# A routed expert layer on one core: gate and up with the weights standing, 160 tokens moving

## The chip, the cores and the metric

The kernel runs on one core of a Trainium2 chip. The metric is the device time of one execution in microseconds. Each number is the median of several runs; one further execution is profiled, and the views shown are of that one.

## The reference

One layer of a decoder on 2048 tokens of width 1024, in float32. What matters here is the middle step, the mixture of experts: 32 experts in 4 groups; each token takes its best group and in it its best two experts. An expert is a gated MLP with a hidden width of 512.

```python
def expert_block(args):
    xblk, e = args
    hdn = jax.nn.silu(xblk @ w_gate[e]) * (xblk @ w_up[e])
    return hdn @ w_down[e]
```

With 2 x 2048 assignments over 32 experts, a mean of 128 tokens falls to one expert. Before it come attention and a short convolution with their projections; after it a gated per-layer embedding and the last norm.

## The kernel before

Everything is computed to nearly float32 precision by splitting each operand into a high part and a low part (both fp32r): `split` makes the high part on ScalarE (L65) and the low part, the difference, on VectorE (L66). A product is then three matmuls: high x high, high x low, low x high (`mm3`, L73 to L75). TensorE holds one operand, loaded by its weight loader (PEld), and moves the other past it.

The stages follow one another: the input projections (`project`), attention (`attention`), the output projection with the router (`mix_out`), a loop for far tokens (`far_experts`), the experts (`experts`), and the rest (`finish`). The order of the work in the expert stage is written out by hand (manual schedule): each engine takes its instructions in the order of the program.

**Experts.** Each expert's three weight matrices are 12 units of 512 KB: units 0 to 3 are gate, 4 to 7 up, 8 to 11 down. SyncE loads units into a ring of 12 raw buffers (L754), a whole expert ahead. `next_unit` splits the next raw unit into a ring of 10 split units (`uh`, `ul`), which frees the raw buffer for the next load. A split waits until TensorE is done with the unit that held its place.

The program holds two bodies for each expert, chosen at run time by the expert's count of tokens: `block(e, True)` for more than 128 tokens, `block(e, False)` for up to 128. The text calls them the wide and the near body. Tokens are listed by expert and rank; GpSimd (POOL) gathers the first 128 rows of an expert into `xg0` and, where the count is over 128, up to 64 further rows into `xg1` (L1220, one gather each). `trans` transposes the first rows (4 transposes to a PSUM tile, L1229) and splits them to `xh` and `xl`. This is done for the next expert within the body of the present one, after units 8 and 9.

In both bodies the tokens stand in TensorE and the weights move: gate by 512 columns, up by 256 (two halves `f` of the hidden width), down by 512, three matmuls for each block. In the wide body the further rows come besides: their transposes at the start of the body (L1356), high and low part side by side as one standing operand of 128 columns, and two matmuls for each block (L1285, L1286); low is added to high afterwards, through `half` (L1250, L1251).

For each half of the hidden width VectorE multiplies up with silu(gate) (`u`, L1299; `sum`, L1296), TensorE transposes the product (L1306, two transposes for the first rows and two for the further ones), and it is split to `hh`, `hl` or `hs` for the down products. `store` copies the result out of PSUM and POOL writes it to `yd`: 128 rows (L1324), and 64 rows (L1322) in the wide body.

Tokens with a rank of 192 and over would go through `far_experts`, a loop over blocks of 128 rows that is entered only if there are any. It scatters its lists with 32 indirect DMAs and adds the results with 32 gathers.

The choice and the order of an expert:

```python
if e + 1 < E:
    with tc.If(self.counts[e + 1] > 128):
        self.gather(e + 1, 1)
n = self.nsplit, self.nload
with tc.If(self.counts[e] > 128) as c:
    block(e, True)
self.nsplit, self.nload = n
with c.Else():
    block(e, False)
```

Of the kernel before, what the change touches and what calls it, by code (L numbers as in the profile page):

```python
# [32 lines left out]

R1 = E * 128
R2 = R1 + E * 64
FAR = 192
# [14 lines left out]
class Kernel:  # L51
# [716 lines left out]

    def next_unit(self, pool=False):
        k = self.nsplit - 12 - 12 * E  # L770
        self.split_unit(self.gcol[:, k:k + 1] if k >= 0 else None, pool)
        self.unit_loads()

    def mix_out(self, st):
# [124 lines left out]
        def route(t0, n):  # L899
# [90 lines left out]
            yield V.tensor_scalar(u1, e_, -64.0, float(R1 - 128), op0=OP.mult, op1=OP.add)  # L990
# [122 lines left out]
        for e in range(2):  # L1113
            self.gather(e, 0)
        self.gather(0, 1)
# [28 lines left out]
        for k in range(2):  # L1144
            self.trans(0, 4 * k, pst)

# [56 lines left out]
    def expert_tiles(self):  # L1203
# [4 lines left out]
        self.idx1 = cp.tile([64, E], I32, name="idx1")  # L1208
        self.xT = [self.xt_pair(cp, 0)]
        self.xg = [[cp.tile([n, D], F32, name=f"xg{r}{i}") for i in range(2)] for r, n in enumerate((128, 64))]  # L1210
# [4 lines left out]
    def xt_pair(self, p, i):  # L1215
        return [p.tile([128, KD, 128], F32R, name=f"{n}{i}") for n in ("xh", "xl")]
# [8 lines left out]
    def trans(self, e, kk, pst):  # L1225
        xh, xl = self.xT[e % 2]
# [3 lines left out]
        self.split(xh[:, kk:kk + 4], xl[:, kk:kk + 4], ps)  # L1230
# [6 lines left out]
    def experts(self, st):  # L1237
        tc, nc = self.tc, self.nc
        V, mm = nc.vector, nc.tensor.matmul
        self.xT.append(self.xt_pair(self.pool(self.est, "e_x1", 1), 1))  # L1240
# [3 lines left out]
        self.banks = [psm.tile([128, 512], F32, name=f"bank{i}") for i in range(6)]  # L1244

        def half(ps, n, out=None):

            lo = wk.tile([64, 512], F32, name="lo", bufs=1)
            r = wk.tile([64, 256], F32, name="sum", bufs=1) if out is None else out
            nc.scalar.activation(lo[:, :n], ps[64:128, :n], AF.Copy)  # L1250
            V.tensor_tensor(r[:, :n], ps[0:64, :n], lo[:, :n], op=OP.add)  # L1251
            return r

        def block(e, more):

            xh, xl = self.xT[e % 2]
            pg, pg1, pu, pu1 = self.banks[0], self.banks[1], self.banks[2::2], self.banks[3::2]
            ys, y1 = self.banks[2:4], self.banks[4:6]
            unit = lambda j: self.units[(10 + 12 * e + j) % NSPLIT]
            hh = wk.tile([128, 4, 128], F32R, name="hh", bufs=1)  # L1260
            hl = wk.tile([128, 4, 128], F32R, name="hl", bufs=1)
            if more:
                xs = wk.tile([128, KD, 2, 64], F32R, name="xs", bufs=1)
                hs = wk.tile([128, 4, 2, 64], F32R, name="hs", bufs=1)

            def free():

                self.next_unit()

            def prods(j, r):  # L1270

                uh, ul = unit(j)
                if j < 4:
                    n, ks, nk, out = 512, (2 * j, 2 * j + 1), KD, [(pg, pg1)[r]]
                elif j < 8:
                    f, i = divmod(j - 4, 2)
                    n, ks, nk, out = 256, range(4 * i, 4 * i + 4), KD, [(pu, pu1)[r][f]]
                else:
                    n, ks, nk, out = 512, (j - 8, j - 8), 4, (ys, y1)[r]
                for i, k in enumerate(ks):  # L1280
                    ps = out[i % len(out)][:, :n]
                    wh, wl = uh[:, i * n:i * n + n], ul[:, i * n:i * n + n]
                    if r:
                        s = xs[:, k] if j < 8 else hs[:, k]
                        mm(ps, s, wh, start=k == 0, stop=False)  # L1285
                        mm(ps, s, wl, start=False, stop=k == nk - 1)  # L1286
                    else:
                        s = (xh[:, k], xl[:, k]) if j < 8 else (hh[:, k], hl[:, k])
                        self.mm3(ps, [(*s, wh, wl)], start=k == 0, stop=k == nk - 1)

            def hidden(f, r):

                fs = slice(f * 256, f * 256 + 256)
                if r:
                    u = half(pu1[f], 256)[:, :256]
                    V.tensor_tensor(u, u, sl1[:, fs], op=OP.mult)  # L1296
                else:
                    u = wk.tile([128, 256], F32, name="u", bufs=1)
                    V.tensor_tensor(u, pu[f][:, :256], sl[:, fs], op=OP.mult)  # L1299
                return u  # L1300

            def hidden_trans(f, r, u):
                n = 64 if r else 128
                ps = self.pst.tile([128, 4, 128], F32, name="tr")[:, :2, :n]
                for k in range(2):
                    nc.tensor.transpose(ps[:, k], u[:, k * 128:k * 128 + 128], self.ident[:n, :n])  # L1306
                K = slice(2 * f, 2 * f + 2)
                if r:
                    self.split(hs[:, K, 0], hs[:, K, 1], ps)
                else:  # L1310
                    self.split(hh[:, K], hl[:, K], ps)

            def store(r):
# [14 lines left out]
            def first(j):  # L1328
# [9 lines left out]
                if j == 11:  # L1338
                    store(0)
# [419 lines left out]
```

## Time and profile before

| | before |
|---|---|
| median of 3 runs | 2375.61 us (2374.02 to 2383.3) |
| the profiled execution, its own time | 2378.32 us |
| its span in the profile | 2376.6 us |
| expert stage, first store to last | 1297.3 to 2136.6 us |
| experts with the wide body / the near body | 16 / 16 |

The span runs from the first to the last instruction of the profile; the own time holds a little around it. In the views, PE is TensorE's matmuls, PEld its weight loads, DVE VectorE, ACT ScalarE, POOL GpSimd and SP SyncE. A matmul's recorded duration includes its way through the pipeline, so that records of one stream overlap; the distance between two starts tells the pace.

### The profile page before, as it was taken

Reading aid. Unit: us, or ns where it says so; the run is one execution under the profiler, and the core shown is the slowest. Engines: PE = TensorE matmul, PEld = TensorE weight load, DVE = VectorE, ACT = ScalarE, POOL = GpSimd, SP = SyncE. Lnnn points to the kernel's source line nnn. Section 1 sums busy time; section 2 is a strip of 40 time slices with the busy share of each in tenths; the row PEclk is TensorE's granted clock in tenths of the full one; section 3 lists DMA queues with packets and bytes.
Section 4 is the critical chain, followed back from the end, with each engine's and each line's share of the span. In section 5 each row is a group of like instructions: output and inputs, shape, how many; then the busy total and the mean of one; then the engine's idle time right before and its main releaser. Section 6 shows DMA issues by size and latency. Waiting matters only on the chain. (4 is left out here: it accounts for less than half of the span.)

```text
span 2376.6 us, 34881 instructions
## 1 busy us (share of the span) xinstructions
PE 2262.7 (95%) x12058; PEld 1869.0 (79%) x12058; DVE 1700.2 (72%) x3109; ACT 1341.3 (56%) x2407; POOL 481.8 (20%) x570
## 2 busy tenths in 40 slices
PE   7999999999999999999988999999999999999997
PEld 6888888888888888778866877787787777778775
DVE  5756666648888888866775777668667776766887
ACT  5334334328888888732236676667556666665443
POOL 0121212022333333401131000101001111003432
PEclk9999999999999999999999999999999999999999
DMA  7363635464556443566647899779777896873552
GB/s 226 100 224 95 223 94 180 110 197 128 134 129 130 90 90 78 133 207 203 205 151 239 293 331 320 230 229 360 230 235 268 288 323 227 290 253 131 173 194 96
DMA packets 297850, 465.68 MB, mean 196 GB/s; under 512 B 27609, under 2 KB 197634, under 8 KB 297602
## 3 DMA queue, kind: packets, MB, share of 16 engines
q1 hardware_dynamic: 253696, 333.43, 45.8%
q0 software_dynamic: 36384, 105.53, 13.6%
q10 hardware_dynamic: 7522, 23.61, 2.7%
q8 instruction: 133, 2.18, 0.4%
q14 instruction: 115, 0.94, 0.2%
HBM read 369.04 MB, written 97.62 MB: 196 GB/s over the span
## 5 line engine op out<-in xcount | busy, mean ns | idle before, releaser
L66 DVE TENSOR_TENSOR ul<-raw,uh 128x1024 fp32r<-128x1024 f32 x396 | 478.6, 1229 | 189.7 <-ACT uh L65 179.5
L65 ACT ACTIVATE uh<-raw 128x1024 fp32r<-128x1024 f32 x396 | 403.2, 1052 | 94.1 <-PE bank L1285 47.5
L73 PE MATMUL bank<-uh,xh 128*128 128x256 f32 (+1 forms) x768 | 252.8, 329 | 21.5 <-ACT uh L65 16.2
L75 PE MATMUL bank<-uh,xl 128*128 128x256 f32 (+1 forms) x768 | 248.3, 323 | 1.2 <-issue 1.2
L74 PE MATMUL bank<-ul,xh 128*128 128x256 f32 (+1 forms) x768 | 248.3, 323 | 1.2 <-issue 1.2
L66 DVE TENSOR_TENSOR pt<-tr,pt 128x512 fp32r<-128x512 f32 (+2 forms) x320 | 194.4, 609 | 60.5 <-ACT pt L65 56.7
L65 ACT ACTIVATE pt<-tr 128x512 fp32r<-128x512 f32 (+2 forms) x317 | 169.0, 534 | 74.3 <-PE tr L653 69.3
L73 PE MATMUL mm<-xh,wh 128*128 128x512 f32 x536 | 210.4, 393 | 0.0
L74 PE MATMUL mm<-xl,wh 128*128 128x512 f32 x536 | 210.2, 392 | 0.0
L75 PE MATMUL mm<-xh,wl 128*128 128x512 f32 x536 | 210.2, 392 | 0.0
L641 ACT ACTIVATE P<-s,mx 128x512 f32<-128x512 f32 (+2 forms) x320 | 199.2, 623 | 17.7 <-DVE mx L632 10.5
L664 PE MATMUL av<-pt,v 128*128 128x512 f32 (+3 forms) x640 | 204.0, 402 | 0.0
L632 DVE TENSOR_REDUCE mx<-s 128x1 f32<-128x512 f32 (+2 forms) x320 | 192.3, 602 | 8.6 <-PE s L629 4.1
L65 ACT ACTIVATE wh<-raw 128x1024 fp32r<-128x1024 f32 x68 | 72.0, 1060 | 216.5 <-PE mm L74 164.9
L73 PEld LDWEIGHTS bank<-uh,xh 128*128 128x128 f32 x768 | 146.7, 191 | 40.5 <-issue 26.7
L653 PE MATMUL tr<-ident,P 128*128 128x128 f32 x1088 | 172.8, 274 | 0.3 <-DVE pt L66 0.3
L75 PEld LDWEIGHTS bank<-uh,xl 128*128 128x128 f32 x768 | 146.6, 191 | 15.1 <-issue 3.1
L74 PEld LDWEIGHTS bank<-ul,xh 128*128 128x128 f32 x768 | 146.8, 191 | 12.7
L1324 POOL DMA_DIRECT2D yd<-y x32 | 18.2, 568 | 675.6 <-ACT y L1320 620.7
L66 DVE TENSOR_TENSOR xl<-tr,xh 128x512 fp32r<-128x512 f32 x160 | 106.1, 685 | 61.5 <-ACT xh L65 57.3
L653 PEld LDWEIGHTS tr<-ident,P 128*128 128x128 f32 x1088 | 128.7, 141 | 24.1 <-DVE pt L66 1.5
L66 DVE TENSOR_TENSOR wl<-raw,wh 128x1024 fp32r<-128x1024 f32 x68 | 82.9, 1220 | 83.2 <-ACT wh L65 81.9
(366 smaller groups left out, 5456.6 us busy)
## 6 DMA issues: line engine op xcount, KB each, us to landing
raw<-in_w_gate_dram SPq DMA_DIRECT2D x128, 512.0 KB, 4.8
raw<-in_w_up_dram SPq DMA_DIRECT2D x128, 512.0 KB, 5.7
raw<-in_w_down_dram SPq DMA_DIRECT2D x128, 512.0 KB, 6.1
raw<-in_w_in_dram SPq DMA_DIRECT2D x68, 512.0 KB, 3.9
yd<-y POOLq DMA_DIRECT2D x32, 512.0 KB, 6.5
xr<-in_x_dram SPq DMA_DIRECT2D x16, 512.0 KB, 6.7
kd<-stg POOLq DMA_DIRECT2D x16, 512.0 KB, 5.4
vd<-stg POOLq DMA_DIRECT2D x16, 512.0 KB, 5.2
```

The source lines that it names most:

```text
L65: nc.scalar.activation(hi, src, AF.Copy)
L66: f = lambda: (lo_eng or nc.vector).tensor_tensor(lo, src, hi.bitcast(F32), op=OP.subtract)
L73: mm(ps, ah, bh, start=(start and i == 0), stop=False)
L74: mm(ps, ah, bl, start=False, stop=False)
L75: mm(ps, al, bh, start=False, stop=(stop and i == n - 1))
L632: nc.vector.tensor_reduce(mx[:, c:c + 1], s, axis=AX.X, op=OP.max, negate=(g == 0))
L641: nc.scalar.activation(G["P"][qi][:, j * 512:j * 512 + s.shape[1]], s, AF.Exp, bias=nm, accum_out=G["rs"][:, qi, j:j + 1])
L653: nc.tensor.transpose(ps[:, jj], G["P"][qi][:, j * 128:j * 128 + 128], self.ident)
L664: mm(G["av"][:, q0:], heads[h]["v"][:, j], G["pt"][jq][:, hl, jj, q0:], start=(j == 0 and hl == 0), stop=(j == 4 * g + 3 and hl == 1))
L1324: nc.gpsimd.dma_start(self.yd[e * 128:e * 128 + 128], y)
```

## The change

- Further rows: up to 32 instead of 64 (`XT`); the main path takes 160 tokens of an expert instead of 192 (`FAR`), and the slots of `yd` follow.
- The transposed tokens of an expert lie in one tile `xT`, high part and low part of 160 tokens side by side for each block of the contraction.
- The near body keeps its products. The transposes of the hidden values use half a bank of their own and come later: the first in the middle of unit 7, the second in the middle of unit 8.
- The wide body is new. For gate and up a block of 128x128 weights stands, and the tokens move: the high part of the weights by 320 columns (both parts of 160 tokens), the low part by 160. The result has the hidden width on partitions; `whole` adds the two halves of the 320 columns, and the product is split without a transpose. Down is computed as before, with 64 standing columns for the further rows' high and low part.
- The next expert's transposes come after units 0, 1 and 2 of the wide body, and after unit 7 and within unit 8 of the near one; with them those of the further rows (`trans_others`), in every expert.
- The gather of further rows is always issued, two experts ahead, without a condition.

```diff
+XT = 32
+FAR = 128 + XT
 R1 = E * 128
-R2 = R1 + E * 64
-FAR = 192
+R2 = R1 + E * XT
...
-            self.gather(e, 0)
-        self.gather(0, 1)
+            for r in range(2):
+                self.gather(e, r)
...
+        self.trans_others(0, pst)
...
+    def xt_tile(self, p, i):
+
+        return p.tile([128, KD, 2, FAR], F32R, name=f"xT{i}")
...
+    def trans_others(self, e, pst):
+
+        X = self.xT[e % 2]
+        ps = pst.tile([128, KD, XT], F32, name="tr")
+        for k in range(KD):
+            self.nc.tensor.transpose(ps[:, k], self.xg[1][e % 2][:, k * 128:k * 128 + 128], self.ident[:XT, :XT])
+        self.split(X[:, :, 0, 128:], X[:, :, 1, 128:], ps)
...
+        banks = [psm.tile([128, 2, 512], F32, name=f"bank{i}") for i in range(3)]
+        free = self.next_unit
+
+        def tiles():
+
+            return (wk.tile([128, 4, 2 * FAR], F32R, name="H", bufs=1),
+                    wk.tile([128, 4, FAR], F32, name="sil", bufs=1))
+
+        def next_trans(e, i):
+
+            if e + 1 < E:
+                if i < 2:
+                    self.trans(e + 1, 4 * i, self.pst)
+                else:
+                    self.trans_others(e + 1, self.pst)
...
+        def products(e, j, H, ys, parts=(0, 1)):
+
+            uh, ul = self.unit(e, j)
+            k = j - 8
+            for f in parts:
+                fs = slice(f * 512, f * 512 + 512)
+                self.mm3(ys[:, f], [(H[:, k, :128], H[:, k, FAR + XT:], uh[:, fs], ul[:, fs])], start=k == 0, stop=k == 3)
...
+        def near(e):
+
+            X = self.xT[e % 2]
+            H, sl = tiles()
+            sl = sl.rearrange("p a b -> p (a b)")
+            pg, tr, pu, ys = banks[0][:, 0], banks[0][:, 1], (banks[1][:, 0], banks[2][:, 0]), banks[1]
+            U = []
+
+            def first(j, ks=None):
+
+                uh, ul = self.unit(e, j)
...
+                    n, k0, nk, ps = 512, 2 * j, 2, pg
...
+                    n, k0, nk, ps = 256, 4 * i, 4, pu[f][:, :256]
+                for i in ks or range(nk):
+                    k, ns = k0 + i, slice(i * n, i * n + n)
+                    self.mm3(ps, [(X[:, k, 0, :128], X[:, k, 1, :128], uh[:, ns], ul[:, ns])], start=k == 0, stop=k == KD - 1)
+
+            def hidden(f):
+
+                u = wk.tile([128, 256], F32, name="u", bufs=2)
+                V.tensor_tensor(u, pu[f][:, :256], sl[:, f * 256:f * 256 + 256], op=OP.mult)
+                U.append(u)
+
+            def hidden_trans(f):
+                ps = tr[:, :256].rearrange("p (k q) -> p k q", k=2)
+                for k in range(2):
+                    nc.tensor.transpose(ps[:, k], U[f][:, k * 128:k * 128 + 128], self.ident)
+                K = slice(2 * f, 2 * f + 2)
+                self.split(H[:, K, :128], H[:, K, FAR + XT:], ps)
...
+            free()
+            free()
+            for j in range(7):
+                first(j)
+                if j == 3:
+                    nc.scalar.activation(sl[:, :512], pg, AF.Silu)
+                if j == 5:
+                    hidden(0)
+                free()
+            first(7, (0, 1))
+            hidden_trans(0)
+            first(7, (2, 3))
+            hidden(1)
+            next_trans(e, 0)
+            next_trans(e, 1)
+            products(e, 8, H, ys, (0,))
+            hidden_trans(1)
+            products(e, 8, H, ys, (1,))
+            next_trans(e, 2)
+            free()
+            free()
+            products(e, 9, H, ys)
+            free()
+            products(e, 10, H, ys)
+            products(e, 11, H, ys)
+            store(e, ys)
...
+        def wide(e):
+
+            X = self.xT[e % 2]
+            H, sl = tiles()
+            gate, up, ys, y1 = banks[0:2], (banks[2:3], banks[0:1]), banks[1], banks[2]
+
+            def first(j):
+
+                uh, ul = self.unit(e, j)
+                if j < 4:
+                    k0, nk, nt, out = 2 * j, 2, 4, gate
...
+                    f, i = divmod(j - 4, 2)
+                    k0, nk, nt, out = 4 * i, 4, 2, up[f]
+                for b, ps in enumerate(out):
+                    for i in range(nk):
+                        k = k0 + i
+                        for t in range(2):
+                            c = (i * nt + 2 * b + t) * 128
+                            cs = slice(c, c + 128)
+                            mm(ps[:, t, :2 * FAR], uh[:, cs], X[:, k], start=k == 0, stop=False)
+                            mm(ps[:, t, :FAR], ul[:, cs], X[:, k, 0], start=False, stop=k == KD - 1)
+
+            def whole(out, ps):
+
+                lo = wk.tile([128, 2, FAR], F32, name="lo", bufs=2)
+                nc.scalar.activation(lo, ps[:, :, FAR:2 * FAR], AF.Copy)
+                V.tensor_tensor(out, ps[:, :, :FAR], lo, op=OP.add)
+
+            def hidden(f):
...
+                u = wk.tile([128, 2, FAR], F32, name="u", bufs=2)
+                whole(u, up[f][0])
+                V.tensor_tensor(u, u, sl[:, K], op=OP.mult)
+                nc.scalar.activation(H[:, K, :FAR], u, AF.Copy)
+                for o, i in ((FAR + XT, 0), (FAR, 128)):
+                    n = XT if i else 128
+                    V.tensor_tensor(H[:, K, o:o + n], u[:, :, i:i + n], H[:, K, i:i + n].bitcast(F32), op=OP.subtract)
+
...
+                    mm(y1[:2 * XT, f], H[:, k, 128:FAR + XT], uh[:, fs], start=k == 0, stop=False)
+                    mm(y1[:2 * XT, f], H[:, k, 128:FAR + XT], ul[:, fs], start=False, stop=k == 3)
...
             free()
             free()
+            for j in range(8):
                 first(j)
+                if j < 3:
+                    next_trans(e, j)
+                if j == 3:
+                    for b in range(2):
+                        whole(sl[:, 2 * b:2 * b + 2], gate[b])
+                    nc.scalar.activation(sl, sl, AF.Silu)
+                if j in (5, 7):
+                    hidden((j - 5) // 2)
...
                 free()
+            for j in (8, 9):
+                products(e, j, H, ys)
+                others(j)
                 free()
+            products(e, 10, H, ys)
+            products(e, 11, H, ys)
+            store(e, ys)
+            others(10)
+            others(11)
+            y = wk.tile([XT, D], F32, name="y1", bufs=1)
+            lo = wk.tile([XT, D], F32, name="lo1", bufs=1)
+            for f in range(2):
+                fs = slice(f * 512, f * 512 + 512)
+                nc.scalar.activation(lo[:, fs], y1[XT:2 * XT, f], AF.Copy)
+                V.tensor_tensor(y[:, fs], y1[:XT, f], lo[:, fs], op=OP.add)
...
         for e in range(E):
             if e + 2 < E:
-                self.gather(e + 2, 0)
-            if e + 1 < E:
-                with tc.If(self.counts[e + 1] > 128):
-                    self.gather(e + 1, 1)
+                for r in range(2):
+                    self.gather(e + 2, r)
             n = self.nsplit, self.nload
             with tc.If(self.counts[e] > 128) as c:
-                block(e, True)
+                wide(e)
             self.nsplit, self.nload = n
             with c.Else():
-                block(e, False)
```

## Rows read from the trace of the kernel before

**Rows 1.** The page's first part: busy us, share, instructions of each engine.

```profile
PE 2262.7 (95%) x12058; PEld 1869.0 (79%) x12058; DVE 1700.2 (72%) x3109; ACT 1341.3 (56%) x2407; POOL 481.8 (20%) x570
```

**Rows 2.** Tile `yd`: operation, count, ns least/median/most, first and last start.

```profile
L1324 POOL DMA_DIRECT2D yd<-y x32: 537/572/593, 1297.3 to 2132.1; - x32
L1528 POOL DMA_INDIRECT raw<-yd,slot_i x32: 934/946/1862, 2140.5 to 2309.6; - x32
L1322 POOL DMA_DIRECT2D yd<-y x16: 538/559/571, 1301.8 to 2136.6; - x16
```

**Rows 3.** Windows: length, busy PE, PEld, DVE, ACT, POOL, granted clock, DMA share, GB/s.

```profile
1418.07:1437.45 19.38, 18.04 (x106) 15.09 (x104) 16.68 (x19) 14.96 (x20) 1.60 (x2) 1.00 1.02 364
1437.45:1461.70 24.25, 21.41 (x118) 17.91 (x119) 16.87 (x19) 15.39 (x20) 2.60 (x3) 0.93 0.95 326
1525.15:1558.44 33.29, 31.49 (x186) 26.62 (x185) 21.95 (x28) 20.04 (x29) 4.09 (x5) 1.00 0.70 229
```

**Rows 4.** Timeline of a wide expert: start, duration, engine, line, operation.

```profile
1326.04 0.39 PE L1285 MATMUL bank<-uh,xs 128*128 128x512 f32 x1
...
1327.89 0.39 PE L1285 MATMUL bank<-uh,xs 128*128 128x512 f32 x1
...
1331.18 0.28 PE L73 MATMUL bank<-uh,xh 128*128 128x256 f32 x1
...
1332.60 0.28 PE L1285 MATMUL bank<-uh,xs 128*128 128x256 f32 x1
```

**Rows 5.** Timeline of attention's scores, PE and PEld, 128 columns.

```profile
711.51 0.22 PE L627 MATMUL s<-k,q 96*128 96x128 f32 x1
711.52 0.19 PEld L628 LDWEIGHTS s<-k,q 96*128 96x128 f32 x1
711.58 0.28 PE L628 MATMUL s<-k,q 96*128 96x128 f32 x1
711.63 0.19 PEld L629 LDWEIGHTS s<-k,q 96*128 96x128 f32 x1
...
711.69 0.28 PE L629 MATMUL s<-k,q 96*128 96x128 f32 x1
```

**Rows 6.** Timeline of attention, a 512-column product behind four transposes.

```profile
721.97 0.42 PEld L653 LDWEIGHTS tr<-ident,P 128*128 128x128 f32 x4
...
722.36 0.19 PEld L627 LDWEIGHTS s<-k,q 96*128 96x128 f32 x1
722.38 0.48 PE L627 MATMUL s<-k,q 96*128 96x512 f32 x1
722.47 0.19 PEld L628 LDWEIGHTS s<-k,q 96*128 96x128 f32 x1
722.70 0.40 PE L628 MATMUL s<-k,q 96*128 96x512 f32 x1
```

**Rows 7.** Timeline of PEld in a wide expert: all waits over 0.3 us.

```profile
1543.62 0.20 PEld L1306 LDWEIGHTS tr<-ident,u 128*128 128x128 f32 x2 [1.07 <-DVE u L1299]
...
1550.01 0.20 PEld L1306 LDWEIGHTS tr<-ident,sum 64*128 64x128 f32 x2 [0.81 <-DVE hl L66]
...
1554.64 0.20 PEld L1306 LDWEIGHTS tr<-ident,sum 64*128 64x128 f32 x2 [0.37 <-PE bank L73]
...
1560.74 0.57 PEld L1356 LDWEIGHTS tr<-ident,xg 64*128 64x128 f32 x8 [0.88 <-issue]
```

**Rows 8.** Groups by line in 1240 to 2000 us: busy us, mean ns.

```profile
L66 DVE TENSOR_TENSOR ul<-raw,uh 128x1024 fp32r<-128x1024 f32 x329 | 395.9, 1222 | 161.2 <-ACT uh L65 151.3 <-DMA raw<-in_w_down_dram 4.2 <-DMA raw<-in_w_up_dram 2.2
L65 ACT ACTIVATE uh<-raw 128x1024 fp32r<-128x1024 f32 x329 | 335.3, 1052 | 74.4 <-PE bank L1285 43.2 <-issue 13.7 <-ACT uh L65 5.9
...
L1299 DVE TENSOR_TENSOR u<-bank,sil 128x256 f32<-128x256 f32 x54 | 22.5, 417 | 0.0
...
L65 ACT ACTIVATE hh<-tr 128x256 fp32r<-128x256 f32 x54 | 20.8, 385 | 60.0 <-PE tr L1306 41.1 <-issue 18.9
```

**Rows 9.** Timeline of PEld where a near expert follows a near one.

```profile
1439.93 0.19 PEld L73 LDWEIGHTS bank<-uh,xh 128*128 128x128 f32 x1 [3.93 <-issue]
```

More of the change, by code (lines that the diff above doesn't have):

```diff
@@ L767, in split_unit, with unit @@
         return uh, ul
+    def unit(self, e, j):
+        return self.units[(10 + 12 * e + j) % NSPLIT]
     def next_unit(self, pool=False):
@@ L1207, in expert_tiles @@
         self.idx = cp.tile([128, E], I32, name="idx")
[L1208 to L1210 removed]
+        self.idx1 = cp.tile([XT, E], I32, name="idx1")
+        self.xT = [self.xt_tile(cp, 0)]
+        self.xg = [[cp.tile([n, D], F32, name=f"xg{r}{i}") for i in range(2)] for r, n in enumerate((128, XT))]
         for r in range(2):
@@ L1243, in experts @@
         psm = self.pool(st, "e_psm", 1, space=PSUM)
[L1244 to L1272, printed above, removed]
+        banks = [psm.tile([128, 2, 512], F32, name=f"bank{i}") for i in range(3)]
@@ L1273, in prods @@
                 if j < 4:
-                    n, ks, nk, out = 512, (2 * j, 2 * j + 1), KD, [(pg, pg1)[r]]
-                elif j < 8:
+                    n, k0, nk, ps = 512, 2 * j, 2, pg
+                else:
                     f, i = divmod(j - 4, 2)
-                    n, ks, nk, out = 256, range(4 * i, 4 * i + 4), KD, [(pu, pu1)[r][f]]
-                else:
[L1279 to L1306, printed above, removed]
-                K = slice(2 * f, 2 * f + 2)
[L1308 to L1311, printed above, removed]
@@ L1328, in first @@
-            def first(j):
-                prods(j, 0)
-                if j == 3:
-                    nc.scalar.activation(sl, pg, AF.Silu)
-                if j in (5, 7):
-                    U[j] = hidden((j - 5) // 2, 0)
-                if j in (6, 8):
-                    hidden_trans((j - 6) // 2, 0, U[j - 1])
-                if j in (8, 9) and e + 1 < E:
-                    self.trans(e + 1, 4 * (j - 8), self.pst)
-                if j == 11:
-                    store(0)
-            def others(j):
-                prods(j, 1)
-                if j == 3:
-                    half(pg1, 512, sl1)
-                    nc.scalar.activation(sl1, sl1, AF.Silu)
-                if j in (5, 7):
-                    U[-j] = hidden((j - 5) // 2, 1)
-                if j == 11:
-                    store(1)
@@ L1351, in block @@
-            sl = wk.tile([128, 512], F32, name="sil", bufs=1)
-            if more:
-                sl1 = wk.tile([64, 512], F32, name="sil1", bufs=1)
-                ps = self.pst.tile([128, KD, 64], F32, name="tr")
-                for k in range(KD):
-                    nc.tensor.transpose(ps[:, k], self.xg[1][e % 2][:, k * 128:k * 128 + 128], self.ident[:64, :64])
-                self.split(xs[:, :, 0], xs[:, :, 1], ps)
+                    mm(y1[:2 * XT, f], H[:, k, 128:FAR + XT], uh[:, fs], start=k == 0, stop=False)
```

52 lines of the change are left out of this document (14 added, 38 removed).

## The prediction

> **What bounds the kernel now.** The page first [rows 1]: TensorE is busy 95% of the span, VectorE 72%, ScalarE 56%. That is an average over stages, so the next view is the table of windows, cut at the stores of the experts' results. The POOL rows of those stores [rows 2] also tell the two kinds of expert apart: all 32 store 128 rows, and 16 store further rows as well (I call these wide, the others near). Between the stores of two wide experts in a row lie 33.3 us [rows 3], of which TensorE is busy 31.5, VectorE 22.0, ScalarE 20.0, and DMA is at 0.70. Between two near ones lie 19.4 to 24.3 us, with DMA at 0.95 to 1.02 and TensorE at 18 to 21. So a wide expert is paced by TensorE alone, and a near one by TensorE with the transfers close behind. The change rewrites both.
>
> A matmul's duration in a pipelined stream is no price; the distance between starts is. In a wide expert 8 products of 512 moving columns start within 1.85 us, 0.231 us each, and 12 of 256 within 1.42 us, 0.118 each [rows 4]. A transpose costs 0.10: four of their weight loads precede the next product's load by 0.39 us [rows 6]. A wide expert has 80 products of 512 (18.5 us), 80 of 256 (9.4), 24 transposes (2.4) and four places where the weight loader waits: 1.07, 0.81, 0.37 and 0.88 us [rows 7]. That sums to 33.4, against 33.3 measured, so these prices explain the wide expert.
>
> **The change, part by part, in a wide expert.** Gate and up now hold a 128x128 block of the weights and move the tokens: for 8 row blocks times 8 column blocks, one product of 320 columns (high and low parts of 160 tokens) and one of 160. Removed are 24 + 16 products of 512 and 48 + 32 of 256: 40 x 0.231 + 80 x 0.118 = 18.7 us. Added are 64 pairs. 320 columns lie between 256 and 512: 0.118 + 0.113 x 64/256 = 0.147 us. The 160 columns alone would be 0.076 on the same line, but here the weight load decides. In the scores of attention, products of 128 columns follow one another [rows 5]: the loads start at 711.52 and 711.63 and the products at 711.58 and 711.69, 0.11 us apart, though the first, with its load done early, lets the next start after 0.07. So a load takes 0.11, hidden only behind a product that is longer. Rows 6 show the same from the other side: a 512-column product behind a transpose has its load at 722.36, the next load comes at 722.47, and the next product starts at 722.70, 0.32 us after it and 0.23 after its load was done. And a load does not begin before the product ahead of it has: in rows 5 and 6 none does. So in the pair the load of the second block hides behind the 0.147 of the first, and the load of the next first block has only the 160 columns to hide behind: 0.147 + 0.11 = 0.257 us. 64 pairs make 16.4 us: 2.2 us less than before. The bounds are 0.223 a pair (loads wholly hidden) and 0.443 (none hidden: 0.11 + 0.147 + 0.11 + 0.076). I take 0.257, since rows 5 and 6 show both cases that it is made of.
>
> The hidden values now come out with the hidden dimension on partitions, so 8 transposes go (0.8 us), and with them the waits in front of them, 1.07 + 0.81 + 0.37 = 2.25 us [rows 7]. What replaces them is on ScalarE and VectorE: adding low to high, the product, the split. By the rows of 256 columns, 0.385 on ScalarE and 0.417 on VectorE [rows 8], a quarter more for 320, one half takes two ScalarE and some three VectorE steps, 2.5 us; with one weight split (1.05 and 1.22 us) in front on each engine, 4.8. The first half has units 6 and 7 as cover, 2 x 8 x 0.257 = 4.1 us; the second has units 8 and 9, 20 products of 512, 4.6. At worst 0.9 us are late per expert, 14 us in all; I take nothing, as the splits fill half of each unit's time.
>
> Down keeps its 40 products. The further rows' input transposes stay 8 in number, moved into the expert before, where the tokens were gathered an expert earlier; the load sets their price, so 32 rows cost what 64 did. VectorE keeps 12 splits of 1.22 and about as much else as before, 22 us, under the new 28. The wide expert becomes 9.2 + 16.4 + 1.6 + 0.88 = 28.2 us. The change is 2.2 + 0.8 + 2.25 = 5.2 us per wide expert, 84 us for 16.
>
> **In a near expert** the products stay. The 8 transposes of further rows are now always made: +0.8 us, 13 us for 16. Against that the transposes of the hidden values come later, half a unit (0.7 us) more of products lying ahead of the first and eight other transposes ahead of the second, so the wait on VectorE's product there shrinks. Bounds are 0 and +13 us; I take 0.2 each, +3. The gather of further rows is always issued: 16 more on POOL, whose indirect rows take 0.93 to 1.86 us [rows 2], on an engine busy 20%, and one expert ahead of need. The condition around it goes, with its branch. I price both at nothing; if the gather were late, the eight transposes would wait, the end of a near expert.
>
> **Where an expert begins** there is a wait that no engine explains: 0.88 us between wide experts [rows 7], up to 3.93 at a near one after a near one [rows 9]. The branch between two bodies stays, so I keep them. As DMA carries the same bytes in less time, its share in a wide expert rises from 0.70 to about 0.70 x 33.3 / 28.2 = 0.83, still short of the near ones' 0.95 to 1.02. Bounds: nothing, and 3.05 us for 16, +49.
>
> **Sum.** -84 + 3 = -81 us. The profiled execution took 2378.3 us, 2.7 above the median of the runs; so 2297 on its own terms, and 2295 as a median.
>
> **Rivals.** *Short loads hidden too* (loads run two products ahead): 0.223 a pair, 64 x 0.034 = 2.2 us more per wide expert, 35 in all, 2260. For it: a product of 128 columns did let the next start after 0.07. Against: in rows 5 the second load waits for the first to end.
>
> *Loads not hidden*, the one on the other side: in the stream of pairs each load waits for the product before it to end. 0.443 a pair, 64 x 0.186 = 11.9 us per expert, +190: 2485. It decides from 0.336 a pair (81 us over 1024 pairs, above 0.257). Against it: the 512-column products follow at 0.231, with nothing left for a load of 0.11. The Trainium skill speaks for it (TensorE: Matmul & The Clock Gate, The mechanism, under Part 3): a load is said to overlap running products only on other row groups, and all products here use all rows; by that rule the sum would be 2485, and the stream of 512s in this trace does not agree with it.
>
> *Starts of wide experts as slow as the near ones'*: 3.93 instead of 0.88, up to +49, 2344. For it: the transfers get denser. Against: 0.83 is not 1.0. The Trainium skill (Runtime: NRT & Kernel Launch, Instruction fetch mechanics) says that a taken branch out of the fetched window stalls until its target is fetched; by it such waits remain at every branch; no row here shows a fetch itself.
>
> *The change does not carry its cases*: 160 tokens instead of 192 in the main path, anything beyond in the slow loop, whose 32 scatters and 32 gathers, at the 0.93 us or more of the gathers in [rows 2], alone are 60 us. The reference's routing, counted on its own inputs, has 16 experts over 128 tokens, as many as the wide ones in the trace, and 155 as the largest. So the loop stays empty. And *nothing comes of it*, some engine already pacing the wide expert: against it, VectorE's 22.0 of 33.3 us.
>
> **How the numbers follow.** The forecast has 0.66, hidden loads 0.15, slow starts 0.11, loads in the open 0.05, nothing 0.02, the slow loop 0.01. A measurement tells about 0.5% (12 us) from no change. The first three are faster: 0.92; no difference 0.02; slower 0.06. The range reaches down to hidden loads, 2258, and up over the forecast with the late hidden half (14) and the near experts' transposes (13), to 2325; slow starts in full and the cases above lie outside, 0.19 together.
>
> **What would show it.** Wide to wide, stores 28.2 us apart; starts in the gate products alternating 0.15 and 0.11; no wait ahead of the first down products; near experts unchanged within 0.5 us; DMA near 0.83 in wide experts. Wrong it would be by pairs of 0.22 or above 0.3, a ScalarE or VectorE releaser ahead of the down products, or starts of 2 us and more.

## The result, and the profile after

The changed kernel takes 2300.1 us (median of 4 runs, 2299.27 to 2304.88), the kernel before 2378.68: a ratio of 0.9674, interval 0.9648 to 0.97. The forecast was 2295. The profiled execution took 2304.88 us, the longest of the four; its span is 2303.1, against 2376.6.

The page's engine line, which answers to [rows 1]:

```profile
PE 2204.5 (96%) x12186; PEld 1845.4 (80%) x12186; DVE 1682.8 (73%) x3109; ACT 1323.1 (57%) x2391; POOL 492.1 (21%) x584
```

The shares have hardly moved and the time has: every engine's share is still an average over stages. So the stages come next, cut at the stores of the first rows as in [rows 3]: two near experts that follow near ones, and a wide one behind a wide one.

```profile
core 0: us, PE busy (x) PEld busy (x) DVE busy (x) ACT busy (x) POOL busy (x), PEclk, DMA share, GB/s
1367.44:1388.13 20.69, 20.31 (x121) 17.11 (x122) 17.02 (x19) 15.80 (x21) 3.81 (x4) 1.00 0.98 352
1388.13:1407.84 19.71, 18.29 (x113) 15.41 (x111) 16.83 (x19) 15.54 (x21) 3.75 (x4) 1.00 1.01 363
1504.86:1533.53 28.67, 27.61 (x185) 24.67 (x184) 20.64 (x27) 18.43 (x26) 4.17 (x5) 1.00 0.76 257
```

The wide expert went from 33.29 to 28.67 us, with VectorE and ScalarE slightly less busy than before. Here are its pairs of products, from TensorE's timeline:

```profile
1509.11 0.35 PE L1370 MATMUL bank<-xT,uh 128*128 128x320 f32 x1
1509.30 0.24 PE L1371 MATMUL bank<-xT,ul 128*128 128x160 f32 x1
1509.37 0.34 PE L1370 MATMUL bank<-xT,uh 128*128 128x320 f32 x1
1509.56 0.24 PE L1371 MATMUL bank<-xT,ul 128*128 128x160 f32 x1
1509.63 0.35 PE L1370 MATMUL bank<-xT,uh 128*128 128x320 f32 x1
...
1510.66 0.35 PE L1370 MATMUL bank<-xT,uh 128*128 128x320 f32 x1
```

Six pairs start in 1.55 us: 0.258 us a pair. The first half of a pair is 0.19 and the second 0.07, not 0.15 and 0.11, and the weight loads show why the sum is still that:

```profile
1509.04 0.19 PEld L1370 LDWEIGHTS bank<-xT,uh 128*128 128x128 f32 x1
1509.15 0.19 PEld L1371 LDWEIGHTS bank<-xT,ul 128*128 128x128 f32 x1
1509.30 0.19 PEld L1370 LDWEIGHTS bank<-xT,uh 128*128 128x128 f32 x1
1509.41 0.19 PEld L1371 LDWEIGHTS bank<-xT,ul 128*128 128x128 f32 x1
```

The low block's load follows 0.11 after the high one's; the high one's follows 0.15 after the low one's, at the time at which the low product starts (1509.30 in both). A load is at most one product ahead.

In that wide expert the weight loader has one wait left, at its start. ScalarE's timeline of the same place stands below it.

```profile
1507.35 0.19 PEld L1370 LDWEIGHTS bank<-xT,uh 128*128 128x128 f32 x1 [1.25 <-ACT lo L1423]
```

```profile
1505.37 0.59 ACT L1423 ACTIVATE lo<-bank 32x512 f32<-32x512 f32 x1 [0.81 <-issue]
1506.71 0.59 ACT L1423 ACTIVATE lo<-bank 32x512 f32<-32x512 f32 x1 [0.74 <-DVE y L1424]
```

This load is the first for the second gate bank, after four pairs for the first one. It starts 0.05 us after the second copy ends: ScalarE takes the low halves of the further rows' results of the expert before out of PSUM in two copies, and the second waits for VectorE's add of the first. By the kernel's text these results lie in another bank (`banks[2]`) than the one that the load waits for (`banks[1]`, the first rows' results of the expert before, whose copies at L1286 were long done). So it is shown that the load waits for the copy, not why it must. The four waits of [rows 7] are gone.

Over all experts, the weight loader's waits, grouped by line and releaser (sum in us, times, longest): before, then after.

```profile
PEld tr L1306 <- DVE u L1299: 35.3, 48, 1.4
PEld bank L73 <- issue: 26.7, 14, 3.9
PEld tr L1306 <- DVE hl L66: 12.2, 15, 0.8
...
PEld tr L1306 <- PE bank L73: 5.9, 16, 0.4
```

```profile
PEld bank L74 <- issue: 22.2, 13, 2.9
PEld bank L1370 <- ACT lo L1423: 10.0, 8, 1.3
PEld bank L1318 <- ACT uh L66: 8.6, 5, 2.8
PEld bank L75 <- issue: 5.7, 1, 5.7
```

Waits ahead of the hidden values' transposes (L1306, now L1318) fell from 53.4 to 8.6 us. The starts of near experts (issue, at the first lines of their products) kept what they had: 29.8 us before, 3.1 of them in a row at L75 that is left out here, and 28.5 after, 0.6 of them at L76.

**Where the time went**, by the distance from store to store, for the expert before and the expert itself:

| | first store | wide after wide, 8 | wide after near, 7 | near after near, 9 | near after wide, 7 | last store to end |
|---|---|---|---|---|---|---|
| before, us | 1297.29 | 33.37 each | 29.47 | 22.33 | 22.95 | 244.5 |
| after, us | 1289.11 | 28.67 | 25.72 | 20.65 | 24.92 | 244.3 |
| change, all | -8.2 | -37.6 | -26.3 | -15.0 | +13.8 | -0.2 |

These make the 73.5 us of the spans. The two columns of mixed neighbours must be shifted before they are read: in a wide expert 12 products of the further rows stood behind that store, now 8 do. 4 x 0.231 [rows 4] x 7 is 6.5 us that moved from the one column to the other. So a wide expert behind a near one lost 32.8 us in 7, or 4.7 each, just as behind a wide one; and the near ones behind wide ones cost 20.3 us more, 2.9 each, while those behind near ones cost 1.7 less.

### The profile page after: what moved, and what is told of

Read it like the earlier page. It is cut to its first block, busy times and chain, and to the rows that moved or that the text cites. A ratio compares the mean times of both kernels' runs of the same rounds, so it can differ in the third digit from the quotient of the medians.

```text
span 2303.1 us, 34960 instructions
## 1 busy us (share of the span) xinstructions
PE 2204.5 (96%) x12186; PEld 1845.4 (80%) x12186; DVE 1682.8 (73%) x3109; ACT 1323.1 (57%) x2391; POOL 492.1 (21%) x584
## 5 line engine op out<-in xcount | busy, mean ns | idle before, releaser
L67 DVE TENSOR_TENSOR ul<-raw,uh 128x1024 fp32r<-128x1024 f32 x396 | 469.5, 1227 | 126.2 <-ACT uh L66 119.9
L66 ACT ACTIVATE uh<-raw 128x1024 fp32r<-128x1024 f32 x396 | 398.3, 1052 | 45.9 <-issue 20.6
L1370 PE MATMUL bank<-xT,uh 128*128 128x320 f32 x1024 | 276.1, 351 | 11.6 <-ACT lo L1423 8.5
L1371 PE MATMUL bank<-xT,ul 128*128 128x160 f32 x1024 | 243.4, 238 | 0.0
L74 PE MATMUL mm<-xh,wh 128*128 128x512 f32 x536 | 210.5, 393 | 0.0
L75 PE MATMUL mm<-xl,wh 128*128 128x512 f32 x536 | 210.2, 392 | 0.0
L76 PE MATMUL mm<-xh,wl 128*128 128x512 f32 x536 | 210.2, 392 | 0.0
L1370 PEld LDWEIGHTS bank<-xT,uh 128*128 128x128 f32 x1024 | 193.5, 189 | 16.3 <-ACT lo L1423 10.0
L1371 PEld LDWEIGHTS bank<-xT,ul 128*128 128x128 f32 x1024 | 196.9, 192 | 0.7
L74 PE MATMUL bank<-uh,xT 128*128 128x256 f32 (+1 forms) x384 | 126.4, 329 | 16.9 <-issue 11.5
L75 PE MATMUL bank<-ul,xT 128*128 128x256 f32 (+1 forms) x384 | 124.0, 323 | 5.2 <-issue 5.2
L76 PE MATMUL bank<-uh,xT 128*128 128x256 f32 (+1 forms) x384 | 124.2, 324 | 0.2 <-issue 0.2
```

The lines of the kernel that those rows point to most:

```text
L66: nc.scalar.activation(hi, src, AF.Copy)
L67: f = lambda: (lo_eng or nc.vector).tensor_tensor(lo, src, hi.bitcast(F32), op=OP.subtract)
L74: mm(ps, ah, bh, start=(start and i == 0), stop=False)
L75: mm(ps, ah, bl, start=False, stop=False)
L76: mm(ps, al, bh, start=False, stop=(stop and i == n - 1))
L1370: mm(ps[:, t, :2 * FAR], uh[:, cs], X[:, k], start=k == 0, stop=False)
```

## The experiments

The first question was the pair: what sets 0.258?

**low240.** The low product moves 240 columns instead of 160 (80 columns of low tokens come in).

```diff
-mm(ps[:, t, :FAR], ul[:, cs], X[:, k, 0], ...)
+mm(ps[:, t, :240], ul[:, cs], X[:, k].rearrange("p a b -> p (a b)")[:, :240], ...)
```

> The product of the weights' low part moves 240 columns instead of 160 (the 80 columns more are low times low of the first tokens and belong to the full product). Theory: in the pair the 160 columns hide behind the next weight load of 0.11 us, and 240 columns would take 0.111, so nothing changes: a pair stays at 0.258, wide experts 28.7 us apart, total 2300 (2296 to 2305). Rival, columns have their price from the first: +0.035 us for each of 1024 pairs, +36, wide to wide 30.9, total 2336.

2301.0 us, ratio 0.9691 (0.9661 to 0.9721); wide after wide 28.75. The 80 extra columns are free but for 0.08 us in 64 pairs: behind a 160-column product the next load is the longer of the two. With 240 columns the starts alternate by 0.14 and 0.11:

```profile
1510.35 0.31 PE L1370 MATMUL bank<-xT,uh 128*128 128x320 f32 x1
1510.49 0.27 PE L1371 MATMUL bank<-xT,ul 128*128 128x240 f32 x1
1510.60 0.31 PE L1370 MATMUL bank<-xT,uh 128*128 128x320 f32 x1
```

**low320.** The low product moves all 320 columns.

```diff
-mm(ps[:, t, :FAR], ul[:, cs], X[:, k, 0], ...)
+mm(ps[:, t, :2 * FAR], ul[:, cs], X[:, k], ...)
```

> The product of the weights' low part moves all 320 columns. Theory: 0.147 us is more than the load of 0.11, a pair becomes 0.294, +0.037 for each of 1024 pairs: +38, wide to wide 31.0, total 2338. Rival, columns have their price from the first: +0.071 a pair, +73, total 2373. If something other than load and columns sets the pace of the pair: no change, 2300.

2333.43 us, ratio 0.9816 (0.979 to 0.9841); wide after wide 30.89. Its starts, on TensorE's timeline:

```profile
1559.88 0.31 PE L1370 MATMUL bank<-xT,uh 128*128 128x320 f32 x1
1560.02 0.31 PE L1371 MATMUL bank<-xT,ul 128*128 128x320 f32 x1
1560.17 0.31 PE L1370 MATMUL bank<-xT,uh 128*128 128x320 f32 x1
1560.32 0.31 PE L1371 MATMUL bank<-xT,ul 128*128 128x320 f32 x1
```

Three distances make 0.44 us: a 320-column product is 0.147, its load hidden, and a pair 0.293. 64 x (0.293 - 0.258) = 2.2 us is the step from 28.67 to 30.89. So the price of a product here is the larger of its columns and the next load's 0.11.

**cond_gather.** The gather of further rows gets its condition back.

```diff
-for r in range(2):
-    self.gather(e + 2, r)
+self.gather(e + 2, 0)
+with tc.If(self.counts[e + 2] > 128):
+    self.gather(e + 2, 1)
```

> The gather of further rows is issued only where the expert has over 128 tokens, as before the change, but two experts ahead. Theory: the condition costs TensorE nothing, the waits at the start of an expert come from the branch between the bodies: 2300 (2296 to 2305). Rival: the condition was what delayed near experts that follow near ones; nine such pairs of stores were 22.3 us apart before the change and are 20.7 now; by it they go back, +15, total 2315.

2303.66 us, ratio 0.9694 (0.9661 to 0.9726); near after near 20.71, wide after wide 28.67. The condition costs nothing that can be measured, and neither do 16 gathers more.

**near_no_others.** Near bodies without the further rows' transposes.

```diff
             products(e, 8, H, ys, (1,))
-            next_trans(e, 2)
             free()
```

> Leaves out the transposes of the next expert's further rows in the near bodies, so that a wide expert after a near one takes old tokens as its further rows. Theory: a near expert is paced by TensorE, and the 8 transposes cost 0.75 us in each of 16: -12, total 2288. Rival: a near expert is paced by the transfers, the transposes lie in time that was waited anyway: 0, total 2300.

2296.52 us, ratio 0.9657 (0.9631 to 0.9682). Of the 12 us that 8 transposes at 0.1 should be worth in 16 bodies, 3.6 came, and the interval overlaps that of the changed kernel. The mean of near after near is 20.89, no less than 20.65; near after wide went from 24.92 to 23.93. Two windows of near experts behind near ones tell more than the mean:

```profile
1382.66:1401.56 18.90, 18.90 (x112) 16.40 (x111) 16.40 (x18) 15.16 (x20) 3.75 (x4) 1.00 1.02 364
1420.40:1443.26 22.86, 20.86 (x115) 18.00 (x116) 16.78 (x18) 15.38 (x20) 2.66 (x3) 0.93 0.99 356
```

Four of the nine windows hold no start wait; they are 18.81 to 18.90 us long, where the least in the changed kernel is 19.63: the eight transposes are paid there too, 0.8 us, and the transfers do not cover them. But four others hold start waits of over 3 us; there the granted clock was 0.86 to 0.93 and TensorE busy for 20.9 to 22.5 us, while in the changed kernel all nine windows are at 1.00. The lower clock took most of the gain back. So the first account is right about the price, and the total can't show it.

**swap_bodies.** The near body comes first in the code, the wide one behind it.

```diff
-with tc.If(self.counts[e] > 128) as c:
-    wide(e)
+with tc.If(self.counts[e] < 129) as c:
+    near(e)
 self.nsplit, self.nload = n
 with c.Else():
-    near(e)
+    wide(e)
```

> The near body stands first in the program and the wide one is jumped to. Theory: the unexplained waits at the start of near experts (28 us over 14 of 16 in the changed kernel) come from the taken branch over the other body; they then move to the wide experts, the near ones start with at most 0.5 us, and the total may go either way by 15 (2285 to 2315). Rival: they come from the dense transfers while near experts run; then near starts keep some 2 us each, wide to wide stays 28.7, total 2300 (2296 to 2305).

2360.45 us, ratio 0.992 (0.9892 to 0.9948): 60 us more than the changed kernel, which neither side expected. The weight loader's waits in it:

```profile
PEld bank L1370 <- issue: 33.9, 7, 7.6
PEld bank L1318 <- ACT uh L66: 14.1, 7, 2.4
PEld bank L74 <- issue: 13.4, 7, 2.9
```

The first row holds 6.75 us of the first expert. Wide after wide is unchanged at 28.67: in either order of the code, one jump over the near body lies between two wide experts. Near after near has one jump over the wide body in either order and keeps 13.5 us of waits. The mixed neighbours tell. Wide after near went from 25.72, with no jump, to 32.76: there the near body ends with a jump over the wide one, and the jump over the near one follows at once. The waits are not the whole price: the granted clock of these seven windows is 0.86 to 0.95, where it was 1.00. Near experts behind wide ones, where no jump is left, start without a wait, but take 24.11 us all the same, since 14.1 us now stand in the middle, at L1318 (the second row; see near experts below). So the order of two bodies with the same work decides 60 us, and the long waits sit where the wide body is jumped over. The denser transfers, the rival, don't explain it: the DMA share in the seven windows is 0.55 to 0.79.

**lo_once.** One copy and one add for the further rows' results.

```diff
-for f in range(2):
-    fs = slice(f * 512, f * 512 + 512)
-    nc.scalar.activation(lo[:, fs], y1[XT:2 * XT, f], AF.Copy)
-    V.tensor_tensor(y[:, fs], y1[:XT, f], lo[:, fs], op=OP.add)
+nc.scalar.activation(lo, y1[XT:2 * XT], AF.Copy)
+V.tensor_tensor(y, y1[:XT], lo, op=OP.add)
```

> The further rows' result leaves PSUM with one ScalarE copy and one VectorE add over both halves instead of two of each in turn. Theory: the 1.25 us that TensorE waits in a wide expert after a wide one are a wait for ScalarE's last copy of the expert before; that copy then ends 0.9 us earlier, wide to wide 27.8, -7 for eight such pairs and up to -13 with the near experts behind wide ones: 2287 to 2293. Rival: the wait is the branch's, as the 0.88 us of the kernel before: wide to wide stays 28.7, total 2300.

2295.55 us (2290.04 to 2299.34), ratio 0.9647 (0.9622 to 0.9672); wide after wide 27.77, as expected. The wait at the start of a wide expert fell with the copy, from 1.25 to 0.35, so it was what the row said. The total is above the 2287 to 2293 expected, and its interval overlaps that of the changed kernel; the gain is shown by the distance.

**others_first.** lo_once, and in a wide expert the further rows' last products come ahead of the first rows' last ones.

```diff
 products(e, 10, H, ys)
-products(e, 11, H, ys)
-store(e, ys)
 others(10)
 others(11)
 ...
+products(e, 11, H, ys)
+store(e, ys)
```

> As with one copy, and the further rows' last products stand before the first rows' last ones, so that their copy lies beside products and ScalarE's last work of an expert is the copy of the first rows. Theory: TensorE's wait falls to the 0.4 us that a wide expert after a near one shows: wide to wide 27.8, total 2287 to 2293; the near experts behind wide ones wait longer for nothing else. Rival: the wait stays at 1.25, 2300.

2286.85 us (2285.53 to 2292.64), ratio 0.9614 (0.9591 to 0.9637): the fastest version that keeps all products, faster than the kernel before and, with an interval that lies below that of the changed kernel (0.9648 to 0.97), faster than that too. The start of a wide expert now waits for the last copy of the first rows alone:

```profile
PEld bank L1370 <- ACT y L1286: 5.6, 15, 0.4
```

No store of first rows has further products behind it now, so the mixed columns are not to be compared with those above; all 31 distances sum to 754.6 us, 769.7 in the changed kernel.

**near_old_order.** The near body of the changed kernel with its transposes at the old places.

```diff
-for j in range(7):
+for j in range(8):
     first(j)
...
+    if j == 6:
+        hidden_trans(0)
...
-first(7, (0, 1))
-hidden_trans(0)
-first(7, (2, 3))
-hidden(1)
+products(e, 8, H, ys)
+hidden_trans(1)
 next_trans(e, 0)
-next_trans(e, 1)
-products(e, 8, H, ys, (0,))
-hidden_trans(1)
-products(e, 8, H, ys, (1,))
-next_trans(e, 2)
...
 products(e, 9, H, ys)
+next_trans(e, 1)
+next_trans(e, 2)
```

> The near body's transposes stand where they stood before the change (hidden values right behind units 6 and 8, the next expert's rows behind units 8 and 9); all else as changed. Theory: the waits ahead of the hidden transposes come back, some 0.7 to 1 us, in near experts behind wide ones and less in a row of near ones, which the transfers pace: +5 to +12, total 2305 to 2312. Rival: the order is worth nothing, since the transfers pace every near expert: 2300 (2296 to 2305).

2320.54 us, ratio 0.9747 (0.9721 to 0.9772): 20 us more than the changed kernel, against 5 to 12 expected.

```profile
PEld bank L1318 <- issue: 16.1, 9, 3.3
PEld bank L1368 <- ACT lo L1421: 15.9, 8, 2.0
...
PEld bank L1318 <- DVE u L1312: 8.3, 13, 0.8
```

Near after near goes to 21.82, 1.17 more each; the wait for VectorE's product is back. What was not expected is the second row: wide after wide, whose body is untouched, goes from 28.67 to 29.15, its start wait from 1.25 to 1.99. It now stands in front of the first gate bank's pairs, four of which ran ahead of it before; why it moved there is not shown. Of the 16.1 us at L1318 without a releaser, 14.1 lie in near experts behind wide ones; in the two longest, 3.3 and 3.2, VectorE's product stood behind seven weight splits in a row.

**before_spread.** The converse: the kernel before, its near body's transposes at the later places.

```diff
 def first(j):
+    if not more and j == 7:
+        prods(j, 0, (0, 1))
+        hidden_trans(0, 0, U[5])
+        prods(j, 0, (2, 3))
+        U[7] = hidden(1, 0)
+        return
+    if not more and j == 8:
...
+        prods(j, 0, (0,))
+        hidden_trans(1, 0, U[7])
+        prods(j, 0, (1,))
+        return
```

> The kernel before, with the near body's transposes of the hidden values and of the next expert's tokens at the later places of the changed kernel, and nothing else. Theory (the later transposes made the near experts faster): near after near goes from 22.33 to about 21.1 us, near waits ahead of the hidden transposes fall by 1 us an expert, wide after wide stays at 33.4; time 2378 less 11 to 20, 2358 to 2367 us. Rival (the near experts gained from something else that changed, such as the length of the body that they jump over): near after near within 0.3 us of 22.33, time within 4 us of the kernel before.

2363.35 us against 2380.4, ratio 0.9931 (0.991 to 0.9953); near after near 21.38, near after wide 21.93. The later transposes by themselves are worth 17 us, a fifth of the whole change. Some 3 of them lie where none were expected: wide after wide fell from 33.37 to 32.97.

**before_xt32.** The kernel before with 32 further rows.

```diff
+XT = 32
-R2 = R1 + E * 64
-FAR = 192
+R2 = R1 + E * XT
+FAR = 128 + XT
```

> The kernel before with 32 instead of 64 further rows per expert, and nothing else. Theory: the 192-row limit cost nothing in the products (their moving columns are the weights), so wide after wide stays at 33.4 us within 0.2; what goes is two of four clearings of the result rows ahead of the experts and half of the further rows' stores: the first store comes 1 to 3 us earlier, time 2374 to 2378 us. Rival (the whole 8.2 us ahead of the first store come from the smaller number of rows): first store 7 to 9 us earlier, time 2368 to 2371.

2370.7 us against 2380.4, ratio 0.996 (0.9944 to 0.9976). The first store comes at 1291.93, 5.4 us earlier, between what the two accounts gave; the time, 9.7 us less, is in the rival's range. Wide after wide is 33.07, 0.3 less where 0.2 was allowed, so the products cost nearly what they did. The read of the further rows' list is at 1246.11 instead of 1249.42: 3.3 of the 5.4 were won ahead of the experts, where two clearings of 1.17 us each went.

**short_wide.** The wide body without its low products in gate and up, for the length of the code that is jumped over.

```diff
-mm(ps[:, t, :2 * FAR], uh[:, cs], X[:, k], start=k == 0, stop=False)
-mm(ps[:, t, :FAR], ul[:, cs], X[:, k, 0], start=False, stop=k == KD - 1)
+mm(ps[:, t, :2 * FAR], uh[:, cs], X[:, k], start=k == 0, stop=k == KD - 1)
```

> Leaves out the products of low weights with high tokens in gate and up of the wide body, so that this body is 64 products and 64 weight loads shorter (174 matmul rows become 110). A near expert begins with the jump over it. Theory (the stall at a near expert's start is the jump over a long body): the unexplained waits of the near experts' first loads, 28.3 us over 14 starts in the changed kernel, fall to under 12 us in all, and a near expert after a near one from 20.65 to 19.5 to 20.2 us. Rival (the stall comes with the dense transfers, whose weight units are late): the transfers get denser still, the waits stay at 2 us a start or grow, near after near stays at 20.6 or more. Both: the 64 products of 320 columns follow at about 0.15 us instead of 0.258 a pair, so wide after wide goes from 28.7 to about 21.8 us, or to 22 to 23 where the transfers now pace it; time 2195 to 2230 us.

2279.28 us, ratio 0.9575 (0.9549 to 0.96). The waits, and one group of weight loads for gate or up in a wide expert:

```profile
PEld bank L74 <- ACT H L1383: 58.5, 20, 3.7
...
PEld bank L75 <- issue: 4.1, 2, 3.5
PEld bank L74 <- issue: 3.8, 11, 1.2
```

```profile
1532.18 2.35 PEld L1370 LDWEIGHTS bank<-xT,uh 128*128 128x128 f32 x16 [0.60 <-DVE sil L1376]
```

At L74 and L75 the near starts cost 27.9 us without a named releaser in the changed kernel; here such waits are 7.9. Near after near is 19.64, with its transfers as dense as ever (a mean DMA share of 1.02 against 0.99). The rival falls: those waits belong to the jumped-over body. That its length alone sets them is not shown. The wide body of the kernel before has as many matmuls by its windows, and the nine starts of near experts behind near ones waited 23.2 us there against 14.6 in the changed kernel; and leaving products out also moves all code behind them. The forecast of the time missed: wide after wide is 27.94, not 21.8 to 23. The products did run at 0.147 (16 loads in 2.35 us), which is 7.1 us less in 64. Most of that comes back as waits: the first down product waits some 3.6 us for ScalarE's hidden values, about 1 us ahead of the further rows' transposes goes to VectorE's split of the tokens, and VectorE is busy 20.6 of 27.4 us in such an expert.

## Why the prediction was right

**The pair.** 0.257 was forecast and 0.258 measured; low240 and low320 show that the mechanism, a load of 0.11 that a product hides or doesn't, is the right one. Loads wholly hidden (0.223) and in the open (0.443) both fall. The rule of the Trainium skill (TensorE: Matmul & The Clock Gate, The mechanism, under Part 3), by which loads overlap running products only on other row groups, does not agree with these rows: here they share all rows, and a load starts with the product ahead of it. Only the pattern was off: 0.19 and 0.07 instead of 0.15 and 0.11. With 240 columns it is as forecast (low240); why the pair divides otherwise with 160 these rows don't settle.

**A wide expert's sum.** 28.2 was forecast, 28.67 measured: 9.24 + 64 x 0.258 + 1.6 + 1.25 is 28.6. The 2.25 us of waits went, as priced. The term that was mis-sized is the start wait, kept at 0.88 and measured at 1.25. It was read as a wait that no engine explains, though in four of the eight such starts the trace before names a releaser, TensorE's own product (L1286, 0.77 us). After the change it is ScalarE's copy chain, by its row and by lo_once.

**The hidden half, 0.9 late at most, taken as nothing.** No wait stands there in the row of the wide expert. short_wide shows that the cover was needed: with units 6 and 7 in 2.4 us instead of 4.1, the wait is some 3.6, more than the cover that went, so the chain on VectorE and ScalarE grew there too.

**Near experts, +0.2 each.** This step failed in its parts, and its sum held by luck: +3 was forecast, and -15.0 + 20.3 = +5 measured. Behind a near expert 1.7 us were won where 0.2 more were forecast; the waits for VectorE's product had been 8.9 us in those nine, and near_old_order and before_spread show 1.17 and 0.95 us each from the transposes' places alone. Behind a wide expert 2.9 were lost, for which the prediction had no term but the eight transposes. Here is one of these in the changed kernel, then one in others_first:

```profile
1845.15 8.04 DVE L67 TENSOR_TENSOR ul<-raw,uh 128x1024 fp32r<-128x1024 f32 x7 [1.92 <-ACT uh L66]
1853.10 0.41 DVE L1312 TENSOR_TENSOR u<-bank,sil 128x256 f32<-128x256 f32 x1
1853.63 0.20 PEld L1318 LDWEIGHTS bank<-ident,u 128*128 128x128 f32 x2 [2.77 <-ACT uh L66]
```

```profile
1830.58 8.04 DVE L67 TENSOR_TENSOR ul<-raw,uh 128x1024 fp32r<-128x1024 f32 x7 [1.30 <-ACT uh L66]
1838.54 0.42 DVE L1312 TENSOR_TENSOR u<-bank,sil 128x256 f32<-128x256 f32 x1
```

VectorE's product for the hidden values stands behind seven weight splits in a row. In the changed kernel these begin 5.1 us after the store of the wide expert (1840.08), behind the copies and adds of its further rows, and TensorE waits 2.77 us for the product (the row names ScalarE's split; the product ends at 1853.51, the wait at 1853.63). In others_first, where those copies come earlier, they begin 0.5 us after the store (1830.10); no wait of this kind is left, and five of the seven near experts behind wide ones take 19.3 to 20.6 us, where 1.85 us of the difference is the further products that no longer lie behind the store. swap_bodies shows it from the other side: its near experts behind wide ones have no start wait, yet 14.1 us at L1318 instead of 8.5, and cost only 0.8 each less. So the late splits and the eight transposes, more than the start waits, make up the 2.9; no run moves the splits alone.

**Gather and branch, at nothing.** Right for the condition (cond_gather) and for the sum of the start waits (29.8, then 28.5). But they moved. Counted by the expert that starts, those of near experts behind near ones fell from 23.2 to 14.6 us, and those behind wide ones rose from 5.5 to 13.7. Why the two jumps at a near expert behind a wide one cost little before and more now is not settled. swap_bodies and short_wide show that such a wait goes with a jump over the wide body. The Trainium skill (Runtime: NRT & Kernel Launch, Instruction fetch mechanics) says that a taken branch out of the fetched window stalls until its target is fetched, which agrees; no row shows the fetch.

**What was not priced.** 8.2 us ahead of the first store. before_xt32 gives 5.4 of them to the smaller number of rows (clearings, list, and what followed them), and the first wide expert's own saving, 4.7 if it is like the others, more than covers the rest. The forecast had that expert among its 16 and nothing for the rows. So -84 was some -75 (16 x 4.7), +3 was +5, and some -4 came from the rows: about -74, against -81 forecast and 73.5 between the spans. The profiled execution lies 4.8 us above its median, with a wait of 5.67 us in one near start; between the medians lie 78.6.

**DMA.** 0.83 was forecast in wide experts, 0.79 was the mean of the eight behind wide ones.

## What to carry to other kernels

When weights stand and short tokens move, price each product at the larger of its columns and the next product's weight load, by distances of starts in the trace; here the columns up to the load were free. A start wait is not a constant: see whose work ends where the wait ends, put that work earlier, and look whether the start follows. Work at the end of one stage can also hold back an engine that the middle of the next stage needs, as the copies did with the splits. Behind data-dependent branches the order of the bodies can count for as much as the work in them, so time both orders.

## What the runs showed of the hardware

In the changed kernel, eight of the nine near experts behind near ones, where one jump over the wide body (185 matmuls by its window) lies between, waited 0.6 to 2.9 us at their first weight loads, and one did not. Where the jump over the near body follows at once (swap_bodies), the waits were 2.5 to 7.6 us. From one wide expert to the next, over a near body alone, only the wait for ScalarE stands, 1.25 us in both orders, which would hide a shorter one; the first expert of swap_bodies, which nothing precedes, waited 6.75. The clock goes with it. After the longest such wait of the changed kernel, 5.67 us at 1346.92, the granted clock was 0.81 of full speed over the next 8 us, a mixture of its levels of 1.2 and 2.4 GHz, with TensorE busy only 2.31 of the 8.03 us ahead of it:

```profile
1338.87:1346.90 8.03, 2.31 (x9) 1.24 (x7) 4.51 (x5) 4.12 (x5) 3.35 (x4) 0.97 0.84 275
1346.90:1355.00 8.10, 8.08 (x40) 7.02 (x41) 3.68 (x4) 4.59 (x5) 0.00 (x0) 0.81 0.75 263
1355.00:1367.44 12.44, 11.10 (x72) 9.15 (x72) 10.27 (x14) 8.54 (x14) 0.00 (x0) 1.00 0.78 255
```

And 80 of 240 moving columns were free: low240 moved half as many columns again in 1024 products, and the time did not change beyond its interval.
